# One bound less in an interleaving: the account of TensorE's work holds one slot's worth instead of two

## The chip, the cores and the metric

The kernel runs on one core of one Trainium2 chip. The metric is the device time of one execution in microseconds (us); the median of several executions counts.

## The reference, cut to what matters

A batch of one with 256 tokens of width 1024 goes through two blocks. The first has a gated linear attention mixer (HGRN2 and GLA heads) and a PEER feed-forward layer; the second has four branches (gated delta rule, spatial gating, sliding window attention, attention to a memory), gates and an output projection. The part around which the change lies is the PEER layer, computed for two blocks of 128 tokens:

```python
s = jnp.einsum('thpd,hpnd->thpn', q, sub_keys)            # 8 heads, 2 x 128 keys
s_top, i_top = lax.top_k(s, PEER_TOPK)                    # 16 of each half
best, pos = lax.top_k(cand, PEER_TOPK)                    # 16 of the 256 sums
expert = jnp.take_along_axis(cand_idx, pos, axis=-1)
g = jax.nn.softmax(best, axis=-1)
act = jax.nn.gelu(jnp.einsum('td,thkd->thk', xb, u[expert]), approximate=False)
return jnp.einsum('thk,thkd->td', (g * act), v[expert])
```

Each token picks 8 x 16 rows of u and of v, 1024 numbers each. So 2 x 128 gathers are needed, each of one row of u and of v for 128 tokens.

## The kernel before

The kernel is one program for all engines; generators in Python write the instructions, and the order in which the generators are advanced is the order of the instructions on every engine's queue. The stretch that matters here is the one call `run(gathers(peer(), routes(), rate, shadow()))` (its rate is 0.75, then 0.58, then 0.36 steps a slot).

peer() is the main line. It runs over slots i = 0 to 262. In slot i it issues gather i on GpSimd (line 858, one tile `uv` of 128 x 2048 numbers out of a ring of 6 tiles, of 10 once mixer_out(1) has begun), the product of gather i-4 with the tokens on VectorE (line 886), its gelu and its weight on ScalarE (lines 890 and 891), the diagonal matrix `dg` of gather i-5 on ScalarE (line 897), and the sum for gather i-7 on TensorE (line 909: two products of a diagonal with 512 columns, four matmul records), or, for some gathers, on VectorE (line 903). With the ring of 6 the distances are 3 and 2 in place of 4 and 3. A tile is free for gather i+10 once the sum of gather i has read it. In the slots 246, 248, 250 and 252 the main line also cuts a weight tile of the next stage into two parts (cut: a cast on ScalarE, line 216, and a subtraction on VectorE, line 217).

routes() chooses the experts (PEER's scores for the first token block, and the selection with its small vector instructions for both). shadow() is the other work: the rest of the mixer of the second token block (mixer_levels(1), mixer_out(1)), peer_norm(1), the PEER scores of the second token block, the projections of the memory, and of the second network's first token block pre2(0), small_proj(0), qkv(0), q_proj twice, deltanet(0), then sliding(0) and memory_attn(0) together, and last pre2_cut(0), a cut of hT for the projections that come first behind the gathers. Where a generator yields, one step ends. A step that yields a number of us asks for a pause of that many us, counted in slots of SLOT_US = 2.7.

gathers() decides slot by slot whether a step of shadow() is written. Each piece of code that issues matmuls may call pe(us), which adds to state["pe"]: 1.8 for a sum on TensorE, 0.9 for a matmul of proj_tok (a step has two), 0.244 for one of proj_chan (a step has eight, together 1.95), 1.1 for four transposes, 1.6 for a level of mixer_levels, 4.0 in all for the first step of mixer_out(1). deltanet, sliding, memory_attn and small_proj book nothing. At the end of each slot the account `credit` is raised by SLOT_US less what was booked since the last slot, with a limit above and none below; if it is positive, no pause is running, and state["left"] is over LAST = 4, one step of shadow() is written. What is left of shadow() when the main line has ended is written behind it. Behind this call last_out(1) adds the sums to the tokens (line 952) and the projections "gmu" and "gmv" begin (lines 373 to 375).

Of the kernel before, what the change touches and what calls it, by code (L numbers as in the profile page):

```python
# [29 lines left out]
SLOT_US = 2.7  # L30
# [111 lines left out]
def kernel(ctx, tc, I, out, dbg=None):  # L142
# [54 lines left out]
    state = {"next": 0, "cut": 0, "depth": 8, "ahead": N_PAIR - 2}  # L197
# [723 lines left out]
    def gathers(main, routes, rate, others):  # L921


        credit, due, i, wake, state["pe"] = 0.0, 0.0, 0, 0.0, 0.0
        for waits in main:
            if waits is True:
                if next(routes, True) is True:
                    next(others)
                continue
            due += rate(i)  # L930
            i += 1
            while due >= 1.0:
                due -= 1.0
                next(routes, None)
            credit = min(credit + SLOT_US - state["pe"], 2 * SLOT_US)
            state["pe"] = 0.0
            if credit > 0 and i >= wake and state["left"] > LAST:
                r = next(others, None)
                if r is not None and r is not True:
                    wake = i + r / SLOT_US  # L940
        yield from others
# [699 lines left out]

    state["late"] = 0
    run(gathers(peer(), routes(), lambda i: 0.75 if i < 12 else 0.58 if i < 100 else 0.36, shadow()))
    state["pool"] = True

# [137 lines left out]
```

## Time and profile before

| | us |
|---|---|
| median of 3 runs (1200.31 to 1201.11) | 1200.53 |
| the profiled execution | 1202.76 |
| its span, first to last instruction | 1201.0 |
| busy: TensorE, VectorE, ScalarE, GpSimd | 1063.7, 874.8, 507.0, 314.9 |

The DMA engines moved 376.40 MB, 268.45 MB of it on the queue of the gathers. A line of a timeline gives the start, the time, the engine, the line of the kernel, the operation, its tiles and how many instructions were merged; in square brackets stands the idle time of the engine before it and what ended that. PEld is the loading of weights on TensorE. A line of a group gives the busy time, the mean in ns, and the idle time before.

### The profile page before, as it was taken

To read this page: it belongs to the slowest core of one execution; us is meant where nothing else is said; L and a number is where in the kernel's file an instruction comes from. 1 tells how busy PE (TensorE), PEld (TensorE's weight loads), DVE (VectorE), ACT (ScalarE), POOL (GpSimd) and SP (SyncE) were. 2 spreads that over 40 slices of the span, in tenths; PEclk is the share of its full clock that TensorE was granted. 3 is DMA by queue.
4 is the path that set the end of the run, shared out by engine and by line. 5 is a ranking of instruction groups with operands and counts; after the bars stand their busy time and mean duration, and the time that the engine had idled before them with its cause. 6 is when DMAs were issued, how large, how long until landed. Compare 5 with 4: busy or idle time off the path is not lost.

```text
span 1201.0 us, 14789 instructions
## 1 busy us (share of the span) xinstructions
PE 1063.7 (89%) x4972; PEld 734.1 (61%) x4972; DVE 874.8 (73%) x1876; ACT 507.0 (42%) x1267; POOL 314.9 (26%) x278
## 2 busy tenths in 40 slices
PE   8999979988969886976888888896799999999987
PEld 6887635544437653633555545543369988888876
DVE  6588587887588678879888999974754686456644
ACT  5625233432343342433434634447444444444441
POOL 1000234334435343433343455463200000000000
PEclk9999989989989997988988988998999999999989
DMA  9636599999999999999999999999753844445620
GB/s 366 214 105 220 202 379 356 360 376 386 426 427 425 424 422 425 426 426 426 425 421 424 399 400 426 416 427 415 281 201 141 298 158 124 129 157 188 191 90 35
DMA packets 68075, 376.40 MB, mean 313 GB/s; under 512 B 7696, under 2 KB 8992, under 8 KB 35232
## 3 DMA queue, kind: packets, MB, share of 16 engines
q0 software_dynamic: 36864, 268.45, 54.4%
q1 hardware_dynamic: 29264, 103.56, 24.3%
q10 hardware_dynamic: 1872, 3.44, 0.8%
q8 instruction: 40, 0.66, 0.2%
q14 instruction: 35, 0.29, 0.1%
HBM read 374.38 MB, written 1.05 MB: 313 GB/s over the span
## 4 chain that ended last, share of the span: by engine, by line
PE 44%; DVE 24%; DMA 15%; ACT 6%; issue 6%; POOL 3%; POOLq 0%; ACTq 0%; SPq 0%; DVEq 0%
DMA uv<-in_peer_uv_dram,idx 12%; DVE uv L886 9%; PE acc L909 8%; POOL uv L858 3%; PE gate L373 2%; PE gate L375 2%; PE gate L374 2%; PE pq L414 2%; PE qkv L414 2%; DVE x L903 2%; DMA w<-in_wts_dram 1%; PE lv L620 1%; DVE ti L769 1%; PE up L373 1%; PE up L374 1%
## 5 line engine op out<-in xcount | busy, mean ns | idle before, releaser
L909 PE MATMUL acc<-uv,dg 128*128 128x512 f32 x836 | 427.8, 649 | 104.1 <-ACT dg L897 97.9
L858 POOL DMA_INDIRECT uv<-in_peer_uv_dram,idx x256 | 301.6, 1178 | 429.5 <-PE acc L909 273.7
L886 DVE SCALAR_TENSOR_TENSOR uv<-uv,hn 128x1024 f32<-128x1024 f32 x256 | 307.6, 1220 | 68.8 <-DMA uv<-in_peer_uv_dram,idx 64.2
L909 PEld LDWEIGHTS acc<-uv,dg 128*128 128x128 f32 x836 | 160.0, 206 | 287.9 <-issue 144.8
L890 ACT ACTIVATE ge<-act 128x1 f32<-128x1 f32 x256 | 51.8, 202 | 372.1 <-DVE uv L886 360.7
L217 DVE TENSOR_TENSOR wp<-w,wp 128x1024 fp32r<-128x1024 f32 x108 | 129.3, 1221 | 76.2 <-ACT wp L216 76.2
L216 ACT CAST wp<-w 128x1024 fp32r<-128x1024 f32 x108 | 109.9, 1051 | 57.2 <-PE up L375 17.7
L897 ACT ACTIVATE dg<-mats,wv 128x128 f32<-128x128 f32 x209 | 81.3, 389 | 3.9 <-PE acc L909 2.4
L295 POOL TENSOR_TENSOR rsb<-rsa,mhalf 128x1 f32<-128x1 f32 (+2 forms) x8 | 7.3, 908 | 283.9 <-DVE rsa L292 283.9
L891 ACT ACTIVATE wv<-ge,gw 128x1 f32<-128x1 f32 x256 | 75.4, 295 | 8.5
L414 PEld LDWEIGHTS pq<-hnT,w 128*128 128x128 f32 x512 | 60.6, 192 | 9.7 <-issue 8.8
L903 DVE SCALAR_TENSOR_TENSOR x<-uv,wv,x 128x1024 f32<-128x1024 f32 x47 | 60.2, 1282 | 3.0 <-ACT wv L891 2.9
L414 PE MATMUL pq<-hnT,w 128*128 128x128 f32 x512 | 61.5, 276 | 0.6 <-DVE hnT L362 0.6
L373 PE MATMUL gate<-wp,hh 128*128 128x512 f32 x128 | 51.8, 405 | 0.0
L414 PEld LDWEIGHTS qkv<-hT,w 128*128 128x128 f32 x384 | 46.9, 198 | 6.8 <-issue 6.6
L375 PE MATMUL gate<-wp,hl 128*128 128x512 f32 x128 | 50.0, 391 | 0.0
L374 PE MATMUL gate<-wp,hh 128*128 128x512 f32 x128 | 50.0, 390 | 0.0
L414 PE MATMUL qkv<-hT,w 128*128 128x128 f32 x384 | 46.9, 281 | 0.0
L323 POOL TENSOR_TENSOR rst<-rst,mhalf 128x1 f32<-128x1 f32 x5 | 2.8, 558 | 149.1 <-DVE rst L322 149.1
L1065 DVE SCALAR_TENSOR_TENSOR qkvT<-qkvr,chan,qkvT 128x128 f32<-128x128 f32 x72 | 24.0, 351 | 5.7 <-ACT qkvT L1063 4.0
L375 PEld LDWEIGHTS gate<-wp,hl 128*128 128x128 f32 x128 | 24.0, 188 | 5.2
L890 ACT ACT_TABLE_LOAD x21 | 26.9, 1283 | 0.4
(501 smaller groups left out, 1787.2 us busy)
## 6 DMA issues: line engine op xcount, KB each, us to landing
w<-in_wts_dram SPq DMA_DIRECT2D x188, 512.0 KB, 5.0
uv<-in_peer_uv_dram,idx POOLq DMA_INDIRECT x256, 11.6
wsm<-in_w_small_dram ACTq DMA_DIRECT2D x8, 132.0 KB, 19.7
x<-in_x_dram SPq DMA_DIRECT2D x2, 512.0 KB, 4.3
skT<-in_skT_dram ACTq DMA_DIRECT2D x2, 512.0 KB, 9.1
mem<-in_mem_dram SPq DMA_DIRECT2D x2, 512.0 KB, 10.0
out_dram<-o SPq DMA_DIRECT2D x4, 256.0 KB, 2.0
row_n<-in_gains_dram ACTq DMA_DIRECT2D x1, 512.0 KB, 5.8
```

The lines of the kernel that those rows point to most:

```text
L216: S.copy(hi, x)
L217: (eng or V).tensor_tensor(out=lo, in0=x, in1=hi.bitcast(F32), op=OP.subtract)
L373: TE.matmul(ps, fh, sh, start=start, stop=False)
L374: TE.matmul(ps, fh, sl, start=False, stop=False)
L375: TE.matmul(ps, fl, sh, start=False, stop=stop)
L414: TE.matmul(ps, wt(g, c)[:, s], x, start=c == 0, stop=c == KC - 1)
L858: G.indirect_dma_start(out=t, out_offset=None, in_=I["peer_uv"], in_offset=bass.IndirectOffsetOnAxis(ap=idx[b][:, h, s:s + 1], axis=0))
L886: V.scalar_tensor_tensor(t, t, 1.0, hn[b], op0=OP.mult, op1=OP.mult, accum_out=act[:, h, s:s + 1])
L890: S.activation(ge, act[:, h, s:s + 1], AF.Gelu)
L897: S.activation(dg[diags], ident, AF.Copy, scale=wv[diags])
L903: V.scalar_tensor_tensor(xr[b], t, wv[sums], xr[b], op0=OP.mult, op1=OP.add)
L909: TE.matmul(acc[b][:, nh], dg[sums], t[:, nh * 512:(nh + 1) * 512], start=start, stop=h == 7 and s == 15)
```

## The change

The limit of the account in gathers() is one SLOT_US instead of two. Nothing else is edited.

```diff
             while due >= 1.0:
                 due -= 1.0
                 next(routes, None)
-            credit = min(credit + SLOT_US - state["pe"], 2 * SLOT_US)
+            credit = min(credit + SLOT_US - state["pe"], SLOT_US)
             state["pe"] = 0.0
             if credit > 0 and i >= wake and state["left"] > LAST:
                 r = next(others, None)
```

## Rows read from the trace of the kernel before

**Rows 1.** Stretch, us, busy us of PE, PEld, DVE, ACT, POOL; granted clock, DMA share, GB/s.
```profile
284.00:656.00 372.00, 314.56 (x1279) 187.65 (x1278) 294.54 (x719) 138.44 (x454) 147.13 (x127) 0.91 1.01 425
656.00:680.00 24.00, 22.02 (x118) 14.98 (x116) 21.84 (x51) 14.63 (x36) 10.51 (x11) 1.00 0.99 393
...
692.00:716.00 24.00, 23.85 (x84) 14.18 (x84) 23.32 (x63) 8.96 (x31) 14.60 (x11) 0.83 0.99 393
...
776.00:836.00 60.00, 48.37 (x163) 24.89 (x162) 40.15 (x83) 31.80 (x101) 29.02 (x24) 0.98 1.01 427
836.00:863.00 27.00, 22.87 (x80) 12.07 (x78) 13.95 (x22) 15.13 (x38) 7.93 (x7) 0.92 0.93 355
863.00:877.80 14.80, 10.86 (x18) 4.03 (x18) 13.41 (x20) 4.75 (x18) 0.00 (x0) 0.77 0.08 33
877.80:1000.00 122.20, 119.94 (x806) 108.48 (x805) 73.28 (x148) 55.99 (x106) 3.86 (x5) 1.00 0.59 205
```

**Rows 2.** Timeline of VectorE in the first attention steps, 814 to 827 us.
```profile
814.38 1.23 DVE L886 SCALAR_TENSOR_TENSOR uv<-uv,hn 128x1024 f32<-128x1024 f32 x1 [1.20 <-DMA uv<-in_peer_uv_dram,idx]
...
816.97 0.79 DVE L1375 COPY_PREDICATED_SCALAR sws<-mats,neg 128x512 f32 x1 [1.36 <-ACT sws L1374]
...
818.44 1.22 DVE L886 SCALAR_TENSOR_TENSOR uv<-uv,hn 128x1024 f32<-128x1024 f32 x1
...
823.57 0.79 DVE L1375 COPY_PREDICATED_SCALAR sws<-mats,neg 128x512 f32 x1 [3.90 <-ACT sws L1374]
...
826.00 1.25 DVE L886 SCALAR_TENSOR_TENSOR uv<-uv,hn 128x1024 f32<-128x1024 f32 x1
```

**Rows 3.** Timeline of GpSimd at 839 us: a gather and what it waited for.
```profile
839.42 0.94 POOL L858 DMA_INDIRECT uv<-in_peer_uv_dram,idx  x1 [8.06 <-PE acc L909]
```

**Rows 4.** Timeline of ScalarE in the softmax steps, 828 to 839 us.
```profile
828.13 1.28 ACT L1387 ACT_TABLE_LOAD   x1
...
834.49 0.20 ACT L890 ACTIVATE ge<-act 128x1 f32<-128x1 f32 x1
...
835.33 1.28 ACT L1442 ACT_TABLE_LOAD   x1
...
838.96 0.20 ACT L890 ACTIVATE ge<-act 128x1 f32<-128x1 f32 x1
```

**Rows 5.** ScalarE from 857 to 880 us: the group of L890, and a timeline row.
```profile
L890 ACT ACTIVATE ge<-act 128x1 f32<-128x1 f32 x8 | 1.6, 203 | 10.1 <-DVE uv L886 10.1
...
857.01 1.03 ACT L216 CAST hh<-hT 128x1024 fp32r<-128x1024 f32 x1
```

**Rows 6.** Timeline of TensorE at 364 us: start, us, engine, line, operation, tiles, count.
```profile
364.41 1.88 PE L909 MATMUL acc<-uv,dg 128*128 128x512 f32 x4
366.13 5.52 PE L414 MATMUL pq<-hnT,w 128*128 128x128 f32 x48
```

**Rows 7.** Timeline of ScalarE at 417 us: a gelu and what it waited for.
```profile
416.98 0.20 ACT L890 ACTIVATE ge<-act 128x1 f32<-128x1 f32 x1 [10.57 <-DMA wsm<-in_w_small_dram]
```

**Rows 8.** Timeline of VectorE at the end of the gathers, 849 to 879 us.
```profile
849.62 0.69 DVE L1458 TENSOR_TENSOR ym<-mo,xm_s 128x512 f32<-128x512 f32 x1
...
855.02 1.22 DVE L886 SCALAR_TENSOR_TENSOR uv<-uv,hn 128x1024 f32<-128x1024 f32 x1
...
858.07 1.23 DVE L217 TENSOR_TENSOR hl<-hT,hh 128x1024 fp32r<-128x1024 f32 x1 [1.82 <-ACT hh L216]
859.21 1.22 DVE L886 SCALAR_TENSOR_TENSOR uv<-uv,hn 128x1024 f32<-128x1024 f32 x1
...
863.40 1.22 DVE L886 SCALAR_TENSOR_TENSOR uv<-uv,hn 128x1024 f32<-128x1024 f32 x1
...
864.54 1.22 DVE L886 SCALAR_TENSOR_TENSOR uv<-uv,hn 128x1024 f32<-128x1024 f32 x1
...
877.77 1.28 DVE L952 TENSOR_TENSOR x<-x,acc 128x512 f32<-128x512 f32 x2 [1.27 <-PE acc L909]
```

**Rows 9.** Timeline of TensorE at the end of the gathers, 870 to 878 us.
```profile
870.17 7.56 PE L909 MATMUL acc<-uv,dg 128*128 128x512 f32 x12 [0.59 <-ACT dg L897]
```

## The prediction

> **What bounds the kernel now.** I read the page's shares, then the busy time by stage, then the timelines of the stage that the edit reaches, the gathers (up to 878 us of a span of 1201.0 us; the execution took 1202.76 us). No engine sets the pace of most of that stage. From 284 to 836 us the DMA engines move 425 to 427 GB/s at a share of 1.01 [rows 1], and only a few stretches fall off that: two of 24 us show 393 GB/s [rows 1]. VectorE waits 1.20 us for the landing ahead of a product of 1.23 us [rows 2]: one gathered tile per 2.44 us. In such a stretch a reordering of TensorE's work is worth nothing, however even it becomes. At the end it is different. From 836 us the rate sinks to 355 GB/s, from 863 us nearly nothing is left to fetch, and VectorE is busy 13.4 of the last 14.8 us [rows 1]: there the bound is the handing back and forth of VectorE and ScalarE. A gather at 839 us waited 8.06 us for an accumulation [rows 3], because ScalarE was in softmax steps until 838.96 us [rows 4] and built no diagonal meanwhile. Behind 877.8 us TensorE is busy 119.9 of 122.2 us [rows 1], so what the end of the gathers loses is not regained soon.
>
> **The change part by part.** No instruction is added or removed; steps of shadow() move to later slots, with their DMAs and their places in the queues. So the first term is a count. I went through the 263 slots with the amounts that the code books: 1.8 for an accumulation, 1.95 for a projection of eight matmuls, 1.8 for a pair of proj_tok, 1.1 for transposes, 1.6 for a level of mixer_levels, nothing for deltanet, sliding and memory_attn. A slot adds 2.7. With the limit of 5.4 the account stands at or near it whenever cheap steps preceded, and then pays for six to eight projection slots in a row (each slot with accumulation and projection loses 0.9 to 1.05); with 2.7 it pays for three. Every such run therefore ends sooner and the steps behind it come later. The counts, old and new slot: first projection of mixer_out(1) 50 and 50; peer_norm(1) 66 and 69; memory() 105 and 110; pre2(0) 141 and 147; qkv(0) 149 and 155; delta_gates(0) 182 and 189; the two attentions 240 and 247; pre2_cut(0) 251 and 258. From 182 on nothing is booked but accumulations, the account stays positive under both limits, and the seven slots remain. They just fit: a step is still taken while state["left"] is over 4, up to slot 258. The trace confirms the old count: slot i computes product i-4, so eight gelu must stand behind the cast of pre2_cut in slot 251, and there are eight [rows 5].
>
> Up to slot 50 (before 284 us) both orders are alike, and what the DMA loses there stays. From slot 50 to 246, TensorE's groups cost 1.72 us for an accumulation and 1.79 us for a projection [rows 6], 3.5 us in a slot against 2.44 us of DMA. A run of eight falls 8 us behind, one of three 3 us; the rows show that the gathers in flight cover even the first (425 GB/s in 284 to 656 us [rows 1], which holds most of these runs). The cover fails at the two stretches of 393 GB/s: 24 x (427 - 393)/427 = 1.9 us lost in each. The queries' projections and the table loads of delta_gates, which stand there, keep their order and come seven slots later. A run of projections in the new count is shorter, but the pauses leave 8 projections in 10 slots where there were 8 in 9, and the seven slots before delta_gates now hold more of them. Of the DMAs that move, SP's weight loads go with their steps, the same bytes in the same order; the ten loads that block2_consts issues on ScalarE's queue go from slot 92 to 97, and the gelu behind them, which waited 10.57 us [rows 7] without a loss of rate, waits there instead. So I take 0, between -3.8 (both dips go) and +3 (two dips more of 1.5).
>
> The end is the term that decides. The old order put the softmax steps into slots 240 to 244, where VectorE still waited for landings; the new one has the last deltanet steps there and the softmax in 247 to 251, among the four cuts of the next weights (slots 246, 248, 250, 252), the last products and pre2_cut. Laid out with the rows' durations from the same start, product 237 at 814.38 us [rows 2]: products 238 to 242 at the DMA's pace, 5 x 2.44: product 242 at 826.6. A slot with a cut costs 4.19 us from product to product (855.02 to 859.21 [rows 8]: ScalarE does gelu, weight, diagonal and the cast, VectorE waits for it), a plain one 1.14 [rows 8]. Slot 246: 830.8; 247: 831.9; 248: 836.1, and the first softmax work on VectorE 1.47 (816.97 to 818.44 [rows 2]): product 245 at 837.6. ScalarE then loads tables and does exponentials for 3.63 (835.33 to 838.96 [rows 4]), gelu to diagonal 0.84 (834.49 to 835.33 [rows 4]), a copy of 0.6 (half the cast's 1.03 [rows 5]): 842.7; VectorE's maxima 2.43 (823.57 to 826.00 [rows 2]): product 246 at 845.2. Slot 250 has a cut (849.4; its cast ends at 848.3), then ScalarE's eight exponentials with two loads 6.36 (828.13 to 834.49 [rows 4]): 854.6; 0.84 and 3.63 again: 859.1; 0.73 to the cast and 2.20 from the cast to the next product [rows 5, 8]: product 249 at 862.1. It was at 863.40 [rows 8], so here 1.3 us are gained. From there the old order needs 877.77 - 863.40 = 14.4 us. The new one has in it, besides, pre2_cut's subtraction, 4.19 - 1.14 = 3.05, the attentions' two last products of 0.69 [rows 8], 1.4, and a wait for the matmuls that feed them, taken as 0.7 (half an accumulation; 0 to 1.7). Sum: 862.1 + 14.4 + 5.1 = 881.6 us, 3.8 us later than 877.77. Bounds: with the waits for casts lying under ScalarE's softmax it is +1; if the last twelve matmuls run at 1.2 GHz, which they partly do already (granted clock 0.77 [rows 1]; 7.56 us where twelve at full clock take 5.2 [rows 6, 9]), and the waits add up, +7.
>
> The DMA's own end comes sooner: the stall in slot 250 holds accumulations 246 and later, whose tiles no gather needs any more, so the drop to 355 GB/s, 27 x (427 - 355)/427 = 4.6 us, goes. What is late next is VectorE's chain, which at 882 us is some 20 us behind the last landing; the earlier landing hides behind it. Who waits on all this: last_out(1) and the first gmu projections, which TensorE starts as soon as the accumulation and the halves of hT are there.
>
> **The rivals.** (a) Faster: the end is set by the landings, not by the chain. For it: the rate does fall in 836 to 863 us and a gather waits 8 us [rows 1, 3]. Against it: none of the last products waits for a landing, and VectorE is busy 13.4 of 14.8 us [rows 1]. It decides if the moved steps all lie in idle time; price -4.6, so 1195.9. (b) The two dips heal through the shorter runs: -3.8 + 3.8 = 0, 1200.5. (c) The late steps lie in idle time but landings don't matter either: 1200.5 to 1201.5. (d) TensorE becomes the bound: with shorter runs its granted clock sinks. In 284 to 656 us it is busy 314.6 of 372 us at 0.91 [rows 1]; below 0.91 x 314.6/372 = 0.77 it no longer fits, and at 0.75 it needs 382 us, +10, with the end 1214. The rows don't suggest it, since work per slot is the same. The Trainium skill, "Perfetto Trace Analysis", section "Matmul Optimizations", speaks against the change in this sense: it asks for matmuls back to back in batches because the engine scales with its use. By that rule (d) would hold; the 0.83 to 1.00 of the stages in the trace shows no link with long runs that I can see. (e) The edit does nothing, the account never standing above 2.7: the eight gelu behind the cast speak against it, as under 2.7 there would be one; 1200.5.
>
> **How the numbers follow.** Against the profiled execution: 1202.76 + 3.8 = 1206.6 us. It lies 2.2 us above the median of the runs, 1200.53, so the forecast for the median is 1200.53 + 0 + 3.8 = 1204.3 us. What can be told from no change is 0.2%, 2.4 us. Chances: forecast 0.56 (own range 1201.5 to 1208; 0.50 of it slower by over 2.4 us, 0.06 within); (a) 0.12, faster; (b) 0.14 (0.11 same, 0.03 faster); (c) 0.09 and (e) 0.04, same; (d) 0.05, slower. That makes faster 0.15, same 0.30, slower 0.55. The range takes the forecast's +1 to +7 with the middle term on its lower side (-3, 1198.5) and a little on its upper (1208.5); most of (a) and (d) stay outside.
>
> **What would show it.** In the new trace one gelu, not eight, should stand behind the cast of hT; the first L1123 should follow 186 gelu; the rate should hold 420 GB/s until the last landing, some 4 us sooner; VectorE's L952 should start some 4 us later than 877.77, with the softmax's loads inside the four cuts. The forecast is wrong if L952 comes no later, if the dips of 393 GB/s are gone or new ones stand between 300 and 830 us, or if the stage behind the gathers changes its length by itself.

## The result, and the profile of the changed kernel

| | before, beside it | changed |
|---|---|---|
| median of 9 runs, us | 1201.11 (1200.25 to 1203.19) | 1210.65 (1206.75 to 1216.44) |
| profiled execution, its span | 1202.76, 1201.0 | 1209.39, 1207.6 |

The changed kernel takes 1.0072 of the time of before, with an interval of 1.0056 to 1.0088: 8.6 us more, 6.7 to 10.6 (the two medians of the table are 9.5 us apart, inside that interval). The forecast was 3.8 us more, so the sign was right and the size less than half. The changed runs also lie further apart here, 9.7 us against 2.9; in the repetition below (e2_after) they do not, 4.8 us against 8.6.

By stage, as in [rows 1] (stretch, us, busy us of PE, PEld, DVE, ACT, POOL; granted clock, DMA share, GB/s):

```profile
284.00:656.00 372.00, 309.13 (x1244) 180.37 (x1242) 292.39 (x712) 139.10 (x452) 148.96 (x129) 0.94 1.01 425
...
692.00:716.00 24.00, 19.81 (x64) 10.57 (x64) 21.24 (x67) 14.49 (x38) 11.47 (x10) 0.86 0.96 381
776.00:836.00 60.00, 56.03 (x206) 29.93 (x204) 40.54 (x80) 25.80 (x87) 31.12 (x27) 1.00 1.01 425
836.00:863.00 27.00, 16.48 (x40) 7.89 (x40) 13.15 (x24) 18.98 (x47) 5.18 (x4) 0.75 0.85 358
863.00:877.80 14.80, 10.68 (x44) 7.28 (x44) 11.05 (x18) 6.12 (x19) 0.00 (x0) 0.88 0.00 0
877.80:1000.00 122.20, 117.62 (x766) 105.76 (x766) 74.19 (x148) 54.26 (x105) 3.87 (x5) 0.97 0.57 199
```

Up to 836 us little differs. The 358 GB/s of 836 to 863 us are a mean of two parts:

```profile
836.00:858.00 22.00, 11.74 (x23) 5.65 (x24) 11.38 (x22) 15.85 (x42) 5.18 (x4) 0.72 1.01 424
858.00:863.00 5.00, 4.73 (x18) 2.25 (x17) 1.77 (x2) 3.13 (x7) 0.00 (x0) 0.88 0.16 66
```

The rate holds until 858 us, as forecast, where before it sank from 836 us on and the last transfers landed at some 864 us. So the transfers do end some 5 us sooner, and it brings nothing: VectorE's chain stands some 20 us behind them. Here it is, the timeline of VectorE at the end of the gathers (start, us, engine, line, operation, tiles; in brackets the idle time before it and what ended it), which answers [rows 8]:

```profile
843.15 0.79 DVE L1375 COPY_PREDICATED_SCALAR sws<-mats,neg 128x512 f32 x1 [3.89 <-ACT sws L1374]
...
848.63 1.22 DVE L217 TENSOR_TENSOR wl<-w,wh 128x1024 fp32r<-128x1024 f32 x1 [1.82 <-ACT wh L216]
849.77 1.22 DVE L886 SCALAR_TENSOR_TENSOR uv<-uv,hn 128x1024 f32<-128x1024 f32 x1
...
861.23 1.23 DVE L217 TENSOR_TENSOR wl<-w,wh 128x1024 fp32r<-128x1024 f32 x1 [5.70 <-ACT wh L216]
862.37 1.22 DVE L886 SCALAR_TENSOR_TENSOR uv<-uv,hn 128x1024 f32<-128x1024 f32 x1
...
869.79 0.69 DVE L1458 TENSOR_TENSOR ym<-mo,xm_s 128x512 f32<-128x512 f32 x1 [1.50 <-PE mo L1454]
...
873.24 0.69 DVE L1418 TENSOR_TENSOR yc<-swo,sw_su 128x512 f32<-128x512 f32 x1 [0.42 <-PE swo L1413]
...
876.90 1.23 DVE L217 TENSOR_TENSOR hl<-hT,hh 128x1024 fp32r<-128x1024 f32 x1 [1.82 <-ACT hh L216]
878.04 1.22 DVE L886 SCALAR_TENSOR_TENSOR uv<-uv,hn 128x1024 f32<-128x1024 f32 x1
...
882.34 1.28 DVE L952 TENSOR_TENSOR x<-x,acc 128x512 f32<-128x512 f32 x2 [0.55 <-PE acc L909]
```

The subtraction hl of pre2_cut has one product behind it (878.04), as the count had it, where before had eight [rows 5]. The attentions' steps (L1375, ym, yc) stand among the casts of weights. L952 comes at 882.34, 4.6 us later than before; the forecast was 881.6. That leaves 2.0 us of this execution's 6.6 behind L952. They come at one place, 948 to 955 us. TensorE's timeline there, first of the changed kernel:

```profile
945.45 1.84 PE L1174 MATMUL l2p<-one,X 128*128 128x1 f32 x16
...
948.43 1.91 PE L1372 MATMUL prev<-swk,swq 64*128 64x128 f32 x8
950.27 5.98 PE L414 MATMUL xmq<-hT,w 128*128 128x128 f32 x32
```

then the same instructions of the kernel before:

```profile
940.85 1.84 PE L1174 MATMUL l2p<-one,X 128*128 128x1 f32 x16
...
943.62 1.05 PE L1372 MATMUL prev<-swk,swq 64*128 64x128 f32 x8
944.60 3.84 PE L414 MATMUL xmq<-hT,w 128*128 128x128 f32 x32
```

The same matmuls take 1.91 instead of 1.05 and 5.98 instead of 3.84 us, because the granted clock there was 0.50, that is 1.2 GHz, in the one and 1.00 in the other. This costs 3.2 us on the spot. By difference 1.2 of them come back later; the trace shows a dip of the clock near 1170 us that is shorter than that of before. The first question for the runs was therefore whether the loss belongs to the end of the gathers or to the stage behind, and whether the smaller account costs by itself or only by making the other work late.

### The profile page after: what moved, and what is told of

Same layout as the page of the kernel before. It is cut to its first block, busy times and chain, and to the rows that moved or that the text cites. A ratio compares the mean times of both kernels' runs of the same rounds, so it can differ in the third digit from the quotient of the medians.

```text
span 1207.6 us, 14793 instructions
## 1 busy us (share of the span) xinstructions
PE 1062.7 (88%) x4976; PEld 731.9 (61%) x4976; DVE 874.2 (72%) x1875; ACT 507.4 (42%) x1268; POOL 321.3 (27%) x278
## 3 DMA queue, kind: packets, MB, share of 16 engines
HBM read 374.38 MB, written 1.05 MB: 311 GB/s over the span
## 5 line engine op out<-in xcount | busy, mean ns | idle before, releaser
L858 POOL DMA_INDIRECT uv<-in_peer_uv_dram,idx x256 | 308.0, 1203 | 419.0 <-PE acc L909 263.8
L890 ACT ACTIVATE ge<-act 128x1 f32<-128x1 f32 x256 | 51.8, 202 | 386.9 <-DVE uv L886 366.1
L897 ACT ACTIVATE dg<-mats,wv 128x128 f32<-128x128 f32 x210 | 81.7, 389 | 2.5 <-PE acc L909 1.1
```

Of the source, the lines that this page charges most:

```text
L858: G.indirect_dma_start(out=t, out_offset=None, in_=I["peer_uv"], in_offset=bass.IndirectOffsetOnAxis(ap=idx[b][:, h, s:s + 1], axis=0))
L890: S.activation(ge, act[:, h, s:s + 1], AF.Gelu)
L897: S.activation(dg[diags], ident, AF.Copy, scale=wv[diags])
```

## The experiments

**Is it the account, or the seven slots?** Theory 1: only lateness counts. Two kernels take the two apart: one keeps the account of one slot and gets the slots back by a larger income, the other keeps the account of two and gives the seven slots away. A third goes three slots further ahead than before, a fourth shifts the stage behind by a pure delay. All four ran on one chip; the median of before was 1202.46 us there.

```diff
# e1_income29, on the changed kernel (e1_income31: 3.1)
-            credit = min(credit + SLOT_US - state["pe"], SLOT_US)
+            credit = min(credit + 2.9 - state["pe"], SLOT_US)
# e1_hold7, on the kernel before
-            if credit > 0 and i >= wake and state["left"] > LAST:
+            if not 182 <= i < 189 and credit > 0 and i >= wake and state["left"] > LAST:
# e1_delay, on the kernel before, in last_out()
+        for _ in range(5):
+            V.tensor_tensor(out=junk, in0=x, in1=x, op=OP.mult)
         r = halves_rstd(x, junk, (add, add))
```

> The cap of the change stays at one slot, and the income of a slot is raised from 2.7 to 2.9. By the paper count the other work then ends in slot 251 as before the change, while no slot may hold more than one slot's worth and the next step. Theory 1 (the other work is late, and lateness is all that costs): L952 stands at 877.8 +-1 us as before, and the time is that of before, 1200 to 1203 us. Rival 2 (the smaller account costs by itself, by another packing of TensorE in the gathers): the time stays near that of the change, 1206 to 1212 us. Rival 3 (what the change adds behind the gathers comes from the shift alone): the same time as theory 1, so this run does not tell 1 from 3.

Measured: 1201.34 us (1199.94 to 1203.52), ratio 0.9992 (0.9981 to 1.0003). L952 on VectorE's timeline stands where it stood before:

```profile
877.64 1.28 DVE L952 TENSOR_TENSOR x<-x,acc 128x512 f32<-128x512 f32 x2 [0.91 <-PE acc L909]
```

> The kernel before, account of two slots, with the other work held back in slots 182 to 188: the delta-rule gates come at slot 189 and the attentions at 247, where the change has them, but everything ahead of slot 182 is as before. Theory 1 (lateness alone): L952 at 881.5 to 883 us, and the time of the change, 1206 to 1212 us. Rival 2 (the cap itself costs): close to before, 1200 to 1203 us.

Measured: 1209.11 us, ratio 1.0052 (1.0034 to 1.0071), with L952 1.3 us past the expected range, at

```profile
884.32 1.28 DVE L952 TENSOR_TENSOR x<-x,acc 128x512 f32<-128x512 f32 x2 [2.19 <-PE acc L909]
```

The account without lateness costs nothing; lateness without the account costs what the change costs. Rival 2 falls. In this trace the 323.2 us from L952 to the end of the span are exactly those of before (1201.0 - 877.77), with no stretch at 0.50 between 888 and 1160 us.

> As the first of these, with an income of 3.1: by the paper count the other work ends in slot 248, three slots sooner than before. Theory 1: the pieces of the other work that stand in the last gathers move up by three slots, and L952 comes 1 to 3 us sooner than 877.8; the time is 1197 to 1200 us if the stage behind keeps its length, up to 1204 us if the clock of that stage goes with its start. Rival 2 (the cap costs by itself): 1204 to 1210 us.

Measured: 1204.26 us (1200.73 to 1209.16), ratio 1.0019 (1.0004 to 1.0035), though the traced execution, the shortest of the twelve, had L952 at 875.65. More income did not pay. The busy time by stage says what it costs; the stretch 500 to 656 us, in which before moved 425 GB/s:

```profile
500.00:656.00 156.00, 120.32 (x483) 70.35 (x482) 131.45 (x324) 57.64 (x182) 61.91 (x52) 0.89 1.00 414
...
716.00:764.00 48.00, 38.42 (x154) 23.00 (x153) 46.36 (x109) 20.91 (x67) 25.64 (x19) 0.93 1.00 407
```

156 x (427 - 414)/427 = 4.7 us and 48 x (427 - 407)/427 = 2.2 us of transfers are lost, where before lost 0.7 and none. Product 237 starts at 822.38 us in this trace, 8.0 us later than in that of before; this loss is most of it.

> The kernel before with five more VectorE products (128x1024 of x into a tile that nothing reads before it is written again) ahead of the first addition of L952; the result is unchanged. Last product ends at about 876.5 us, five times 1.14 us make 882.2 us: L952 4.4 us later, as in the change, and nothing else moved. Theory 1 with a stage behind that keeps its length: 1201.1 + 4.4 = 1205.5 us, as close together as the runs of before. Rival 3 (the stage behind loses by the shift itself, through TensorE's clock): 1207 to 1211 us, with a stretch at a granted clock near 0.5 between 940 and 960 us, and a wider spread.

Measured: 1209.91 us, ratio 1.0055 (1.0036 to 1.0075), 4.3 to 9.0 us. VectorE's timeline:

```profile
875.27 2.68 DVE L903 SCALAR_TENSOR_TENSOR x<-uv,wv,x 128x1024 f32<-128x1024 f32 x2
877.98 6.26 DVE L958 TENSOR_TENSOR hn<-x 128x1024 f32<-128x1024 f32 x5
884.35 1.28 DVE L952 TENSOR_TENSOR x<-x,acc 128x512 f32<-128x512 f32 x2
```

The delay is 6.4 us, of which 1.3 lay in the wait for acc that before has [rows 8], so 5.1 were added, and the interval of the time holds that. (The median itself lies in rival 3's range; the low end of the interval reaches theory 1's.) 1.5 us of this execution were late before the delay. The 1.9 us that its stage behind is longer (325.2) come with a granted clock of 0.50 from 890 to 896 us, after TensorE had been idle for 6.7 us. So a delay at L952 is paid in full, and what it costs beyond that is not clear from this run.

**Does the stretch at 0.50 belong to the change?** The changed kernel again, a smaller delay, an earlier end of the other work without touching the account, and the changed kernel without the narrow matmuls ahead of the stretch; the median of before was 1202.75 us.

```diff
# e2_delay2: the delay above with range(2)
# e2_early8, on the kernel before
                 r = next(others, None)
+                if 200 <= i < 208:
+                    r = next(others, None)
                 if r is not None and r is not True:
                     wake = i + r / SLOT_US
# e2_l2p1, on the changed kernel, for the second half of the tokens
-        for i in range(8):
-            TE.matmul(ps[:, 0, i:i + 1], X[:, i], one, start=True, stop=True)
+            TE.matmul(ps[:, 0, 0:8], X[:, 7], one.to_broadcast([P, 8]), start=True, stop=True)
# ... (the loop stays for the first half)
```

> The changed kernel once more, as the control of the other three on their chip and for a second trace of it. Theory 1 (two parts: the end of the gathers comes later, and TensorE's clock falls now here, now there behind it): the median stays 6 to 9 us over before; in the profiled execution the time from L952 to the end of the span is near 323.2 us if TensorE is granted 1.00 from 888 to 1160 us, as in the traces of before and of the kernel that held the other work back, and near 325.2 us if there is a stretch at 0.50 in it, as in the first trace of the change. Rival 2 (the stretch at 0.50 between 948 and 955 us belongs to the change): it is there again at the same place, with 325.2 us.

Measured: 1210.62 us (1206.7 to 1211.54), ratio 1.0061 (1.0044 to 1.0079). In this trace (of the execution of 1206.7 us) L952 is at 881.49 and the span ends 323.4 us later; the stretch that ran at 0.50 in the first trace of the same kernel is at full clock:

```profile
944.00:948.00 4.00, 4.00 (x37) 3.99 (x36) 1.23 (x1) 1.55 (x3) 0.00 (x0) 1.00 0.93 350
948.00:952.00 4.00, 4.00 (x36) 3.85 (x34) 2.99 (x3) 3.53 (x4) 0.00 (x0) 1.00 0.84 264
```

So it does not belong to the change (rival 2 of this run falls).

> As the delay by five products, with two: the last product ends at 876.5 us, 2.3 us more is 1.1 us beyond the wait for acc that ends at 877.8, so L952 comes 1.1 us later. Theory 1, with a stage behind that keeps its length: before plus 1.1 us, 1.000 to 1.002. Rival 3 (any shift against the place of before brings the stage behind out of a favourable place): plus 3 to 5 us, 1.0025 to 1.004.

Measured: 1205.49 us (1200.33 to 1208.83), ratio 1.0018 (1.0003 to 1.0033). Both expectations lie in that interval; the run decides nothing. Its trace had a stretch at 0.5 to 0.6 at 946 to 950 us and 325.0 us behind L952.

> The changed kernel; for the second half of the tokens the eight sums of squares of L1174 (16 records of 128x1, 1.84 us) are made by one matmul of 8 columns, so all eight heads get the norm of the last one. That removes the narrow matmuls just ahead of the place where the first trace of the change showed 0.50. They cost 1.6 us by themselves. Theory 1 in the form that the narrow matmuls bring the fall: no stretch at 0.50 between 940 and 960 us, and 3 to 4 us under the change on the same chip (1.6 us of their own and 2 us of the fall). Rival 4 (the fall comes wherever it comes, whatever is issued there): 1 to 2 us under the change, and falls at other places of the stage as before.

Measured: 1213.06 us, ratio 1.0083 (1.0066 to 1.0101): not less than the changed kernel, but more, and L952, which lies ahead of the edit, at 886.17. A dip to 0.60 at 958 to 962 us came without the narrow matmuls, but behind an idle time of TensorE of 1.71 us that the edit had made. So the theory that the narrow matmuls bring the dip is not borne out, and the run is no clean test of it. What it does show is how far traces of one order of the gathers lie apart: 881.49, 882.34 and 886.17. Part of that goes with the kernel and not with the execution, for the fastest of its six runs (1211.96 us) is slower than the slowest of e2_after's (1211.54 us), although the two are alike up to L952; why is open.

> The kernel before with a second step of the other work in each of the slots 200 to 207 (steps of the delta rule that are booked at nothing): by the paper count the other work ends in slot 243 instead of 251, the attentions begin at 232 instead of 240. Theory 1 (what sets the end of the gathers is how late the softmax steps and the casts lie): L952 comes 3 to 6 us sooner, 872 to 875 us, bounded by the four casts of weights and the last products that stay at the end; time 1196 to 1200 us if the stage behind keeps its length, up to 1203 us with a fall of the clock in it. Rival 2 (the two steps of a slot stall TensorE and VectorE and the gathers run later): L952 at 877 us or later, time 1201 us or more.

Measured: 1201.74 us (1197.72 to 1204.44), ratio 0.9991 (0.9978 to 1.0005), L952's work (line 954 there) at 877.66: no gain. These are rival 2's figures, and the gathers do run later, product 237 at 826.02 us. By stage, two stretches in which before moved 427 and 422 GB/s:

```profile
716.00:764.00 48.00, 38.11 (x171) 24.17 (x170) 42.54 (x98) 17.47 (x56) 19.23 (x16) 0.89 0.94 360
764.00:836.00 72.00, 59.40 (x207) 31.90 (x205) 50.21 (x105) 42.96 (x131) 28.48 (x26) 0.93 0.97 405
...
860.00:868.00 8.00, 4.76 (x10) 1.98 (x11) 6.18 (x10) 3.92 (x13) 1.50 (x1) 0.91 1.01 428
```

48 x 67/427 + 72 x 22/427 = 11.2 us of transfers were lost (0.8 of them before the edit too), where the doubled steps stand (329 GB/s from 720 to 745 us) and where the attentions now stand (311 GB/s from 820 to 828 us), and the transfers run at 428 GB/s until 868 us. The other work costs one way when it is early and another when it is late.

**Is the end one chain of VectorE's in its order?** If so, it must shorten when a wait is taken out of VectorE's queue. The four casts of weights in the last ten slots, and in two kernels the cast of hT in pre2_cut as well, are taken apart: ScalarE rounds, VectorE subtracts one slot later. The median of before was 1204.51 us.

```diff
# e3_split_*: in peer(); cast_to() is cut_to() without the subtraction
-            if n - 10 <= i < n - 2 and i % 2 == 0:
-                cut_to(4 * Z_GU + 1 + (i - n + 10) // 2, V)
-                load_to(4 * Z_GV + (i - n + 8) // 2)
+            if n - 10 <= i < n - 2:
+                if i % 2 == 0:
+                    cast = cast_to(4 * Z_GU + 1 + (i - n + 10) // 2)
+                else:
+                    for x, hi, lo in cast:
+                        V.tensor_tensor(out=lo, in0=x, in1=hi.bitcast(F32), op=OP.subtract)
+                    load_to(4 * Z_GV + (i - n + 8) // 2)
# e3_split5_*: besides, in shadow()
-        pre2_cut(0)
+        hh2[0] = slot3("hh0", 8, P, F32R), slot3("hl0", 8, P, F32R)
+        S.copy(hh2[0][0], hT[0])
+        yield
+        V.tensor_tensor(out=hh2[0][1], in0=hT[0], in1=hh2[0][0].bitcast(F32), op=OP.subtract)
```

> The changed kernel with each of the four casts of weights that peer() does in its last ten slots taken apart: ScalarE rounds in the even slot as now, VectorE subtracts one slot later, so that it has not to stand for the 1.82 us of rounding. Theory 1 (the end of the gathers is one chain of VectorE's in its order, and waits in it cost one for one): four waits of 1.8 us are gone where nothing else holds the products, 3 to 7 us off L952, 875 to 879.5 us, and a time 3 to 7 us under the change: 1203 to 1208 us. Rival 5 (the chain is held by ScalarE's exponentials and gelus, and VectorE's waits only move): within 1.5 us of the change.

Measured: 1206.53 us (1204.45 to 1210.33), ratio 1.0017 (1.0003 to 1.0030) against before, where the change without the edit had 1.0061 and 1.0072: some 5 to 7 us won by the ratios, which come from different chips, and 4.1 us by the medians themselves. The trace does not show that gain at L952, which was expected at 875 to 879.5 us:

```profile
861.61 1.23 DVE L932 TENSOR_TENSOR wl<-w,wh 128x1024 fp32r<-128x1024 f32 x1 [4.56 <-ACT wh L236]
...
881.69 1.29 DVE L967 TENSOR_TENSOR x<-x,acc 128x512 f32<-128x512 f32 x2 [2.25 <-PE acc L920]
```

The changed kernel's own traces had 882.34 and 881.49. From product 237 on it is 66.5 us against their 68.3 and 69.6, so 2 to 3 us are won there. VectorE still stands 4.56 us ahead of the last weight's subtraction, because its cast came behind ScalarE's softmax: in this order rival 5 holds in part.

> The same edit on the kernel before. Theory 1: four waits (5.27, 2.30, 1.83 and 1.82 us at the four weights) shrink by 1.8 us each, as far as the last transfers allow, which end between 860 and 866 us: L952 at 871 to 876 us and a time 2 to 6 us under before, 1195 to 1200 us. Rival 5: within 1 us of before. Rival 3 (a shift of the stage behind costs by itself): L952 sooner, but a time within 2 us of before.

Measured: 1197.59 us, ratio 0.9938 (0.9920 to 0.9957); L952's work at 872.44.

> As the one before, and the cast of hT[0] at the end of the other work taken apart in the same way: one more wait of 1.82 us gone from VectorE's order. Theory 1: L952 another 0 to 1.8 us sooner, time 1194 to 1199 us. Rival 5: as before.

Measured: 1195.15 us (1193.87 to 1199.13), ratio 0.9930 (0.9909 to 0.9951): faster than both kernels. VectorE's timeline of it (L932 and L1658 are the subtractions, L897 the products, L967 is L952's work):

```profile
850.38 1.22 DVE L932 TENSOR_TENSOR wl<-w,wh 128x1024 fp32r<-128x1024 f32 x1
851.52 1.22 DVE L897 SCALAR_TENSOR_TENSOR uv<-uv,hn 128x1024 f32<-128x1024 f32 x1
852.66 1.22 DVE L1658 TENSOR_TENSOR hl<-hT,hh 128x1024 fp32r<-128x1024 f32 x1
853.80 1.22 DVE L897 SCALAR_TENSOR_TENSOR uv<-uv,hn 128x1024 f32<-128x1024 f32 x1
854.94 1.22 DVE L932 TENSOR_TENSOR wl<-w,wh 128x1024 fp32r<-128x1024 f32 x1
...
864.56 1.23 DVE L897 SCALAR_TENSOR_TENSOR uv<-uv,hn 128x1024 f32<-128x1024 f32 x1 [0.28 <-DMA uv<-in_peer_uv_dram,idx]
...
868.93 1.29 DVE L967 TENSOR_TENSOR x<-x,acc 128x512 f32<-128x512 f32 x2 [0.54 <-PE acc L920]
```

The last three subtractions follow a product without a gap, where before VectorE stood 1.8 us ahead of each (ahead of the first two it still waits, 4.12 and 0.68 us against 5.28 and 2.30), and the last product now waits 0.28 us for its landing: the chain has been shortened until the transfers are about to be the bound. In the order of before, theory 1 holds and rival 5 falls. The Trainium skill, "Perfetto Trace Analysis", section "Tensor Engine Instruction (MATMUL, LD_WEIGHTS)", says in a note that VectorE and ScalarE take their work strictly in order; these rows agree, since the product at 849.77 us of the changed kernel came only behind the subtraction that waited 1.82.

> One slot's account with an income of 3.1 (other work over in slot 248 by the paper count) and all five casts taken apart. Theory 1: the 2 us by which the income alone brought L952 forward and what the split casts give add up until the last transfers set the end: L952 at 869 to 873 us, time 1193 to 1198 us if the stage behind keeps its length, up to 1201 us with a fall of the clock in it.

Measured: 1203.79 us, ratio 0.9991 (0.9975 to 1.0007): missed. The last product waits for its landing here too, but 9 us later:

```profile
873.95 1.23 DVE L897 SCALAR_TENSOR_TENSOR uv<-uv,hn 128x1024 f32<-128x1024 f32 x1 [0.65 <-DMA uv<-in_peer_uv_dram,idx]
```

With the chain out of the way, the transfers lost to the early other work set the end.

**Where do the other 4 us sit?** Kernels cut off behind the gathers give the time of many executions of that stage alone (the median of before, uncut, was 1201.8 us).

```diff
# e4_cut_*: everything behind the gathers is replaced by
+    for b in range(NB):
+        if b:
+            V.tensor_tensor(out=xr[1], in0=xr[1], in1=acc[1].rearrange("p a n -> p (a n)"), op=OP.add)
+        nc.sync.dma_start(out=out.rearrange("o (b p) d -> p (o b) d", p=P)[:, b], in_=xr[b])
```

> The kernel before up to the end of the gathers: the addition of acc to x of L952 is done in one piece, both halves of x are written out, and everything behind is left out. By its trace L952 stands at 877.8 us, so the time is about 877.8 + 1.2 (the addition) + 2 to 4 (writing) + 1.5 = 883 to 885 us. It is the base of the other two; by itself it tells only how far apart the executions of the gathers are: within 3 us if the spread of before comes from behind, 6 us or more if it comes from the gathers.

Measured: 887.88 us (884.46 to 889.65), above the 883 to 885 expected; the spread of 5.2 us lies between the two marks and decides nothing.

> The changed kernel cut off at the same place. Theory 1 (the median's 8.6 us are the end of the gathers, which the traced executions show between 3.7 and 8.4 us late): 6 to 8 us over the cut kernel of before. Rival 3 (the end of the gathers is 4 us late as forecast, and the other 4 us come behind it): 3 to 5 us over it.

Measured: 896.21 us (894.15 to 898.17), 8.3 us more, and the two groups of runs don't overlap. The last addition in the two traces, before and then changed (each time is 6.6 us behind its addition):

```profile
877.85 1.22 DVE L1649 TENSOR_TENSOR x<-x,acc 128x1024 f32<-128x1024 f32 x1 [0.90 <-PE acc L909]
```

```profile
891.60 1.22 DVE L1649 TENSOR_TENSOR x<-x,acc 128x1024 f32<-128x1024 f32 x1 [1.69 <-PE acc L909]
```

> One slot's account with an income of 3.1, cut off at the same place. Its trace had L952 2.1 us sooner than before, its median over 12 runs was 1.8 us more. Theory 6 (the sooner work takes transfers in the stretch 500 to 776 us, where its trace shows 414 and 409 GB/s against 425 and 421, so the gathers themselves end no sooner in most executions): 0 to 3 us over the cut kernel of before. Rival 3 (the gathers end 2 us sooner, the stage behind loses 4 us): 1 to 3 us under it.

Measured: 888.20 us (885.95 to 890.33), 0.3 us over the cut kernel of before. That is inside theory 6's range, but the two groups of runs overlap, and rival 3's 1 us under is not excluded.

The loss sits in front of L952; the stage behind adds nothing on average that can be told. With five runs of each and their spread, the 8.3 us are known to about 3 us (an estimate). One reservation: the traced cut kernels are at the low end (884.46) and at the high end (898.17) of their runs, and the cut kernels as a whole end their gathers some 4.5 us later than the uncut ones would (887.9 - 6.6 against 1201.8 - 1.8 - 323.2), so only the difference of the two is read.

## Why the prediction was wrong in size

**The count** was right: seven slots, one product behind pre2_cut, and lateness alone as the cause.

**The middle term, 0.** In the first trace it was right: product 237 starts at 814.06 us against 814.38 [rows 2]. Over five traces with the account of one slot and the income of 2.7 (the changed kernel twice, e2_l2p1, e4_cut_after, e3_split_after) it starts at 814.1, 811.9, 816.8, 820.8 and 815.2, mean 815.8; over six with the account of two up to there (before, both delays, e4_cut_before, both split kernels of before) between 813.8 and 815.8, mean 814.9. That is +0.9, inside the bounds of -3.8 to +3, and too little to be told apart. But the traces of the change lie 9 us apart at this point and the others 2, and from 656 to 776 us, where the dips lie, they move 395 to 410 GB/s against 410 to 415. "Keep their order and come seven slots later" was judged by one execution; that the dips would be less steady was not seen, and why they are stays open. Neither half of the change shows it in its one trace: e1_income29, with the account of one slot alone, has 413 GB/s there and product 237 at 814.67 us, e1_hold7, with the lateness alone, 411 and 814.54.

**The end term, +3.8.** This is the step that failed. By the prediction L952 stands 881.6 - 814.38 = 67.2 us behind product 237. The traces of the new order give 68.3, 69.6, 69.8 (e1_hold7), 69.4 (e2_l2p1) and 70.8 (e4_cut_after), mean 69.6; those of the old order 63.4, 63.0 (e1_income29) and 62.9 (e4_cut_before), mean 63.1. So the term is +6.5. As far as product 249 the layout nearly held: 47.7 us forecast from product 237, 48.1 to 49.6 measured, 0.8 more on average. From there I had 19.5 us: 14.4 of the old order, 3.05 for the cut, 1.4 for the attentions' last products, 0.7 for their waits. The traces have 20.0, 21.5, 21.7, 21.2 and 21.2. Two sizes are off. The waits for the attentions' matmuls, taken as 0.7 "(half an accumulation; 0 to 1.7)", are 1.50 + 0.42 = 1.9 us in the first trace and 2.0 in the other four, past that bound too. And the wait for acc ahead of L952, which I left at the 1.27 us of [rows 8], is 0.55 in the first trace and 1.7 to 2.2 in the other four. With 2.0 and 2.0 in place of 0.7 and 1.27 the same layout gives 21.5. TensorE's timeline shows what both waits hang on, first in the first trace:

```profile
869.59 1.88 PE L909 MATMUL acc<-uv,dg 128*128 128x512 f32 x4
871.31 1.89 PE L1413 MATMUL swo<-swv,swpT 128*128 128x64 f32 x16
...
880.32 1.98 PE L909 MATMUL acc<-uv,dg 128*128 128x512 f32 x4 [2.35 <-ACT dg L897]
```

then the last line's instructions in the second trace of the same kernel (e2_after):

```profile
878.06 3.40 PE L909 MATMUL acc<-uv,dg 128*128 128x512 f32 x4 [2.35 <-ACT dg L897]
```

Ahead of the second of the attentions' products stand a whole accumulation and the sixteen matmuls of swo, not half an accumulation. The last accumulation comes behind the same idle time of 2.35 us in all five traces. In the first it ran at a granted clock of 1.00 and took 1.98 us; in the second the clock was 0.57, most of the time at 1.2 GHz, and it took 3.40, in the other three 3.1 to 3.6. So the longer wait for acc is that accumulation at the low clock; what decides the level there the runs don't show. I had this as the upper bound ("the last twelve matmuls run at 1.2 GHz ... and the waits add up, +7") and took the middle, although the row nearest to it, a clock of 0.77 in the last 14.8 us of before [rows 1], already pointed to the slow side.

**Behind the gathers** the prediction took the same length. Traces say 323.2 us of before against 325.3, 323.4 and, in e1_hold7, 323.2; the cut pair says 8.3 of the 8.6 us lie ahead, to about 3 us. As far as that can tell, the step was right, and the first trace, with its 2.0 us at 948 us, misleads.

**The sum** from the traces is 6.5 + 0.9 = 7.4 us, inside the measured 6.7 to 10.6. **The range** ended at +8.0 for the median because its upper side had only the end term's bound and little of the middle's; the interval of the result lies across that edge.

**The rivals.** (a) falls: the transfers end some 5 us sooner, and no gain; but once the casts are taken apart the landings are about to set the end, at 868.93 in e3_split5_before. (b) falls: of the two dips of 393 GB/s one has risen to 416 (656 to 680 us) and the other fallen to 381 (692 to 716 us), and over 656 to 776 us both first traces move 410. (c) and (e) fall with e1_hold7 and the single product behind hl. (d): the granted clock of 284 to 656 us is 0.94 against 0.91 [rows 1], so it did not sink with shorter runs. By the rule of the Trainium skill, "Perfetto Trace Analysis", section "Matmul Optimizations", it should have; this stage does not show it.

## What to carry to other kernels

Where an account or a budget decides when side work is written, ask first where the side work ends under each setting: a limit that looks like smoothing can be a delay, and then it costs what the work costs at the place where it lands; here that was a chain of in-order engines behind the last transfer, where an added delay was paid one for one (e1_delay), while too early an end took the transfers themselves. At such an end, look for pairs in which one engine stands for another's half of the same step (round here, subtract there) and put a slot of other work between the halves; that won 0.6 to 0.7% on the kernel before, about as much as the change lost. And price an end by several executions or by a kernel cut off there: two traces of one and the same kernel lie 0.9 us apart here (881.5 and 882.3), while a kernel with the same instructions up to that place stands at 886.2.

## What the hardware showed that I had not expected

TensorE's granted clock can fall to 0.50, 1.2 GHz, in the midst of matmuls that follow each other without idle time: 948 to 955 us in the first trace of the change, behind sixteen 128x1 and eight 64-row matmuls, and it was back at 1.00 in the midst of 128-column matmuls. In the second trace of the same kernel, and in that of before, the same instructions ran at 1.00. What decides between them the runs don't show. In four traces that have such a stretch between L952 and 1160 us the span behind L952 is about 2 us longer (325.0 to 325.3 us, against 323.0 to 323.4 in seven without one and 322.1 in e2_early8), but not always: e1_income29 has one at 944 to 948 us and 323.6, and e2_l2p1, with its own edit in that stage, has one and 324.0. In e1_income29 the later dip near 1170 us, at 0.57 for 8 us in before, is short as well (0.75 and 0.83 in two stretches of 4 us), which may have given time back.
